# Two-layer hybrid encoder: the attention half of the mixer's output projection is written beside the last steps of the Hyena filters

## The chip, the cores and the metric

The kernel runs on one core of a Trainium2 chip. The metric is device time in microseconds (us), here the median of a few executions. TensorE (PE) multiplies matrices, VectorE (DVE) and ScalarE (ACT) work on elements, GpSimd (POOL) and SyncE (SP) mostly issue DMAs. Each engine works through its own queue in order.

## The reference, cut to what matters

The input is 1024 tokens by 1024 channels, all float32. Layer 0 mixes tokens with two head groups, attention and RWKV-7, whose outputs are concatenated and go through one projection; layer 1 uses a Hyena operator with long filters that depend on weights alone. Each layer ends with a SwiGLU FFN.

```python
def reference(x, c, ...):
    cond = jax.nn.silu(c)
    for layer in range(DEPTH):
        mod = (cond @ ada_w[layer] + ada_b[layer])[:, None, :]
        shift_m, scale_m, gate_m, shift_f, scale_f, gate_f = jnp.split(mod, 6, axis=-1)
        h = rms_norm(x, norm_mix[layer]) * (1.0 + scale_m) + shift_m
        if layer % 2 == 0:
            y = attention_rwkv_mixer(h, ...)   # concat([y_attn, y_rwkv]) @ w_out
        else:
            y = hyena_mixer(h, ...)            # filt = hyena_filters(l, ...) from weights alone
        x = x + gate_m * y
        h = rms_norm(x, norm_ffn[layer]) * (1.0 + scale_f) + shift_f
        x = x + gate_f * swiglu(h, ffn_w1[layer], ffn_w3[layer], ffn_w2[layer])
    return rms_norm(x, final_norm)
```

## The kernel before, in words

**Operands in two parts.** A large product is made of three matmuls with reduced-precision operands (fp32r): each float32 tile is split into a high part (ScalarE copies, L256) and a low part (VectorE subtracts, L257). `mm3` (L296) multiplies high by high, high by low and low by high.

**Pages.** Working memory is cut into pages of 128 partitions by about 1024 columns: float32 pages as a stack from the left, fp32r pages as a stack from the right. `page` takes the page that has been free longest, `free` puts it back. `repage(nf, nr)` changes how many there are of each kind: pages above the new count, which must be free, are given up, and new ones are made in their place. `fence(dt, n)` sorts the free pages into those numbered below n (`pages`) and the others (`beyond`); `zone` says which of the two lists `page` looks at, and in which order. A new page stands where old ones stood, so its first writer waits for the last use of those.

**Order.** The program is written by generators that yield step by step. `weave` takes several with weights and runs always the one whose count of steps over its weight is smallest. The written order is a priority: the scheduler that lays out each engine's queue may put an instruction ahead of others that are written before it, if its data and its page are there first.

**The mixer.** After the input projection `mixer` sets 42 float32 pages and 4 fp32r pages and splits the eight PSUM banks into two groups of four. RWKV's eight units (four head pairs, two directions) pass through three stages, `rwkv_x`, `rwkv_y` and `rwkv_s`, in nine weaves. Beside them runs `other`: attention, in steps of score blocks, and behind it `hy_filters`, which makes the spectra of layer 1's filters in eight quarters (two orders, four column blocks). A quarter loads raw weights (L1788, on POOL), splits them, makes the taps (matmuls L1805, VectorE L1808), multiplies by four DFT matrices that `load_mats` loaded (L1830, VectorE L1750 and L1751), and ends with an eight-point transform (`dft8`, VectorE L1699 and L1700) whose results POOL's queue stores (`hs`, L1777). The transform of a quarter is written beside the taps of the next, and that of the last quarter stands alone at the end. In the last weave (i = 9) only `rwkv_s` of the last unit and `other` (64 steps at most) are left. `rwkv_post` ends it, with L1544 as its last VectorE operation, and spills the RWKV output (`sp_yr`).

**The projection.** Then `build` repages to 13 float32 and 33 fp32r pages, loads x back in eight tiles (`sp_x`), and runs `project`: it loads and splits the four attention outputs (`sp_ya`), and `matvec_add` loads and splits four weights of 512 by 256 (`in_mix_w_out`, L274) and makes eight output tiles of 24 matmuls each. Each tile ends with two gated residual adds (L801). The RWKV half follows in `halves` (`matvec_halves`, L828), woven with the norm ahead of the FFN.

```python
    K.repage(13, 33)
    xT = [K.unspill(d) for d in xd]
    run(project(xT, ys[:4], w[:512], 0))
    xT, steps = K.ffn(xT, halves(xT, ys[4:], w[512:], 0), 0, ada1(), hy_weights(), 20)
```

`project` is also used in `hyena`, where it is woven with the convolutions (`rest`), and there loads and stores each tile of x by itself.

Of the kernel before, what the change touches and what calls it, by code (L numbers as in the profile page):

```python
# [10 lines left out]
F32 = mybir.dt.float32  # L11
# [10 lines left out]
P = 128  # L22
# [41 lines left out]
def run(gen):  # L64
    for _ in gen:
        pass


def some(gen, n):

    for _ in range(n):
        if next(gen, gen) is gen:
            return
        yield


class Kern:
# [77 lines left out]
    def page(self, shape=(P, 1024), dt=F32):  # L155
        t = next(z[dt] for z in self.zone if z[dt]).popleft()
        return reshape(t[:, : int(np.prod(shape[1:]))], shape)

    def free(self, *aps):
        for a in aps:  # L160
            if isinstance(a, (tuple, list)):
                self.free(*a)
            else:
                dt, t, _ = self.page_of[a.tensor.name]
                assert all(t is not q for q in self.pages[dt])
                self.put(t)
# [39 lines left out]
        (eng or self.nc.sync).dma_start(out=d, in_=t)  # L206
        return d

    def unspill(self, d, eng=None):
        t = self.page()  # L210
        (eng or self.nc.sync).dma_start(out=t, in_=d)
        return t

# [566 lines left out]
        at, n = groups[-1]  # L780
        return xT, self.matvec_halves(xT, w2[at * P : (at + n) * P, :], ys, layer, 5, low)

    def matvec_add(self, xT, w, ys, layer, part, g=0, keep=None):

        nc = self.nc
        nk = len(ys)
        load = lambda mp: self.load_w(w[mp] if isinstance(w, dict) else w[:, mp * 256 : mp * 256 + 256], nk, 256)
        nxt = load(0)
        for mp in range(KT // 2):
            wt = nxt  # L790
            if mp + 1 < KT // 2:
                nxt = load(mp + 1)
            for m in (2 * mp, 2 * mp + 1):
                o = (m % 2) * P
                away = xT[m].tensor.name not in self.page_of
                x = self.unspill(xT[m]) if away else xT[m]
                ps = [self.bank(g) for _ in range(2)]
                self.mm3(ps, [(wt[0][:, k, o : o + P], wt[1][:, k, o : o + P]) for k in range(nk)], ys)
                for n in range(2):
                    xs = x[:, HALVES[n]]  # L800
                    nc.vector.scalar_tensor_tensor(out=xs, in0=ps[n], scalar=self.modc(layer, part, m), in1=xs, op0=ALU.mult, op1=ALU.add)  # L801
                self.fbank(ps)
                if keep is not None:
                    keep.append(x)
                elif away:
                    nc.sync.dma_start(out=xT[m], in_=x)
                    self.free(x)
                yield
            self.free(wt)
# [737 lines left out]
        self.free(y)  # L1547
        return d

    def mixer(self, w, h, ada):  # L1550

        self.rwkv_consts()
        self.set_banks(5, 3)

        units = [{"d": d, "hp": hp} for hp in range(4) for d in range(2)]
        self.scanm = self.page((P, PAGE))
        self.nc.sync.dma_start(out=self.scanm, in_=self.ins["k_scanm"])

        def first():

            while (0, "t") not in self.ready:
                yield "wait"
            yield from self.rwkv_x(units[0], 1)

        tiles = self.rwkv_tiles()
        for i, t in zip((13, 15, 17, 19, 20, 21), self.attn_tiles()):
            tiles.insert(i, t)
        out, ys, outr = {}, {}, {}
        att = self.attention(out, 1)

        def begin():

            while (2 not in self.qd) or units[0].get("W") is None or len(units[0]["W"]) < 2:
                yield
            self.zone = (self.beyond, self.pages)
            next(att)
            self.zone = (self.pages,)
            yield
            next(att)
            yield  # L1580

        begun = begin()
        weave((250, self.stream(w, h, tiles, begun)), (60, ada(1)), (30, first()))
        run(begun)
        for a in h:
            self.free(a)
        self.repage(42, 4)
        self.set_banks(4, 4)

        def beside():  # L1590
            f = self.hy_filters(1)
            for n, _ in enumerate(att):
                yield
                if n in (208, 228, 248):
                    next(f)
            yield from f

        other = beside()
        for i in range(1, len(units) + 2):
            if i == len(units):  # L1600
                self.free(self.scanm)
            n = (0, 46, 37, 37, 37, 37, 37, 36, 35, 64)[i]
            gens = [(n, some(other, n))]
            if i > 1:
                gens.append((23 if i <= len(units) else 34, self.rwkv_s(units[i - 2], ys, outr, 0)))
            if i <= len(units):
                gens.append((36, self.rwkv_y(units[i - 1], 0)))
            if i < len(units):
                gens.append((16, self.rwkv_x(units[i], 0)))
            weave(*gens)  # L1610
        for _ in other:
            pass
        self.set_banks(8)
        return [out[i] for i in range(4)] + [outr[i] for i in range(4)]

# [50 lines left out]
            yield  # L1668
        return hid

    def load_mats(self, name):

        out = []
        for i in range(2):
            t = self.page((P, 4, 256))
            self.nc.gpsimd.dma_start(out=t, in_=self.ins["k_" + name][:, 4 * i : 4 * i + 4, :])
            out.append(t)
        return out
# [75 lines left out]
    def hy_filters(self, g):  # L1754

        nc, i = self.nc, self.ins
        hid = yield from self.hy_hidden(g)
        F = self.load_mats("F") + self.load_mats("Fn")
        tneg = self.const("tneg")
        fo = i["hy_f_out"][0]  # L1760
        self.hspec = {}
# [153 lines left out]
    def hyena(self, w, h, tail):  # L1915
# [140 lines left out]
        def rest():  # L2056
            yield from f
            for a in h:
                self.free(a)
            while len(zs) < 4:  # L2060
                yield
            for n, _ in enumerate(tail(zs[:4])):
                yield 1.0 if n == 0 else 5.3

        f = front()
        run(piece(f))
# [28 lines left out]
def build(ctx, tc, ins, out):  # L2095
    K = Kern(ctx, tc, ins)
    spec = [
        ("c", rows(ins["c"])),
        ("ada_b", rows(ins["ada_b"])),
        ("norm_mix", rows(ins["norm_mix"])),  # L2100
        ("norm_ffn", rows(ins["norm_ffn"])),
        ("final_norm", rows(ins["final_norm"])),
    ]
    K.repage(38, 7)
    cols = K.load_cols(spec + K.attn_spec() + K.rwkv_spec() + K.hy_spec())
    next(cols)
    K.ada_init()
    xT = []

    def ada(g):  # L2110
        for m in range(KT):
            xd.append(K.spill(xT[m], f"sp_x0{m}"))
            K.free(xT[m])
            yield
        for part in range(2, 6):
            yield from K.ada_part(0, part, g, 2)

    def ada1():
        for part in range(6):
            yield from K.ada_part(1, part, 0, 2)  # L2120

    def hy_weights():

        w = ins["hy_w_in"][0]
        for j in range(24):
            hw_in[j * P] = K.presplit(w[:, j * P : (j + 1) * P], KT, P, f"hwi{j}")
            yield
        w = ins["hy_w_out"][0]
        for a in range(2):
            for mp in range(4):  # L2130
                hw_out[a][mp] = K.presplit(w[a * 512 : a * 512 + 512, mp * 256 : mp * 256 + 256], 4, 256, f"hwo{a}{mp}")
                yield

    hw_in, hw_out = {}, ({}, {})

    xd = []
    K.load_xT(ins["x"][0], xT)
    K.ada_first()

    def project(xT, ys, w, layer, g=0):  # L2140

        y = [K.split(K.unspill(d)) for d in ys]
        yield
        yield from K.matvec_add(xT, w, y, layer, 2, g)
        K.free(y)

    def halves(xT, ys, w, layer):

        return K.matvec_halves(xT, w, [K.split(K.unspill(d)) for d in ys], layer, 2)

    K.repage(20, 26)
    low = [K.page(dt=F32R) for _ in range(10)]
    h = K.norm_h(xT, 0, 0, [(n, m) for n in range(2) for m in range(KT)], KT - 1)
    K.free(low)
    run(cols)
    w = ins["mix_w_out"][0]
    ys = K.mixer(ins["mix_w_in"][0], h, ada)
    K.repage(13, 33)
    xT = [K.unspill(d) for d in xd]
    run(project(xT, ys[:4], w[:512], 0))  # L2160
    xT, steps = K.ffn(xT, halves(xT, ys[4:], w[512:], 0), 0, ada1(), hy_weights(), 20)

    xd = [K.dram(f"sp_x1{m}") for m in range(KT)]
    h = K.norm_h(xT, 1, 0, steps, 1, xd)
    K.free(xT)
    K.repage(26, 20)
    ys = K.hyena(hw_in, h, lambda y: project(xd, y, hw_out[0], 1))
    K.repage(13, 33)
    xT = [K.unspill(d) for d in xd]
    xT, steps = K.ffn(xT, halves(xT, ys, hw_out[1], 1), 1)  # L2170
    K.final(xT, steps, out)
    K.free(xT)
    K.close()
# [82 lines left out]
```

## Time and profile before

| | us |
|---|---|
| median of 3 runs | 3384.54 (3375.49 to 3385.33) |
| the profiled execution | 3373.19 |
| its span, first to last instruction | 3371.4 |
| mean granted TensorE clock | 0.963 of full speed |

The profile is of one execution. The page gives the busy time of each engine over the whole span. The views used below are windows (busy time of each engine between two times, with the count of instructions, then the granted TensorE clock, the busy share of the DMA engines and the rate), the chain of waits that ended last (start, length, what it was), and the timeline (start, length, engine, line, operation, output and inputs, count; in brackets the idle time of that engine before it, and what ended it).

### The profile page before, as it was taken

What the parts mean: (1) busy time and instruction counts of PE and PEld (TensorE: products, weight loads), DVE (VectorE), ACT (ScalarE), POOL (GpSimd) and SP (SyncE); (2) the same over time, 40 slices, a digit from 0 to 9 for tenths busy, and PEclk for the clock granted to TensorE, in tenths of its full rate; (3) what the DMA queues carried; (4) which work ended last, traced back from release to release, by engine and by line L of the source; (5) the groups of instructions that cost most, each with busy time, mean ns of one, the idle gap of its engine ahead of it and who ended that gap; (6) DMA issues with size and microseconds to landing.
All of it is one profiled execution on the core that took longest, in us unless ns stands there. A gap on an engine that the chain in (4) does not pass through costs nothing.

```text
span 3371.4 us, 51166 instructions
## 1 busy us (share of the span) xinstructions
PE 3158.1 (94%) x20227; PEld 2554.1 (76%) x20227; DVE 2341.6 (69%) x4011; ACT 1229.9 (36%) x2146; POOL 197.0 (6%) x443
## 2 busy tenths in 40 slices
PE   8899989999989979999999999989977899999998
PEld 4687767776668867888887877877765788888886
DVE  5465565666667895887877665699898686667545
ACT  4632355555554432532233333222120443334211
POOL 2000000000001110000001210000000000000000
PEclk9999999989989999999999999999988999999998
DMA  8654542332334253244449983332446322234311
GB/s 273 220 190 139 158 98 70 84 87 64 76 72 111 98 183 137 94 156 137 147 135 308 352 281 125 100 119 90 148 162 218 132 82 75 77 111 138 122 41 51
DMA packets 331377, 460.24 MB, mean 137 GB/s; under 512 B 101816, under 2 KB 233745, under 8 KB 331136
## 3 DMA queue, kind: packets, MB, share of 16 engines
q1 hardware_dynamic: 292576, 322.04, 31.1%
q0 software_dynamic: 38384, 134.86, 11.4%
q8 instruction: 159, 2.61, 0.3%
q14 instruction: 82, 0.67, 0.1%
q10 hardware_dynamic: 176, 0.07, 0.0%
HBM read 312.71 MB, written 141.56 MB: 135 GB/s over the span
## 4 chain that ended last, share of the span: by engine, by line
PE 58%; DVE 8%; DMA 5%; issue 3%; ACT 2%; POOL 0%; DVEq 0%; SPq 0%; ACTq 0%; POOLq 0%
PE bk L296 21%; PE bk L615 8%; PE bk L616 8%; PE bk L614 8%; PE bk L1830 2%; DVE p L1699 2%; PE bk L1849 2%; DMA p<-in_hy_w_in_dram 1%; DVE p L257 1%; DMA p<-in_ffn_w_dram 1%; PE bk L2002 1%; PE bk L1859 1%; PE bk L1805 1%; PE bk L2025 1%; DMA p<-sp_z 1%
## 5 line engine op out<-in xcount | busy, mean ns | idle before, releaser
L296 PE MATMUL bk<-p,p 128*128 128x512 f32 x5136 | 1235.2, 399 | 75.3 <-ACT p L256 35.0
L296 PEld LDWEIGHTS bk<-p,p 128*128 128x128 f32 x5136 | 974.8, 192 | 299.1 <-ACT p L256 39.3
L256 ACT ACTIVATE p<-p 128x512 fp32r<-128x512 f32 (+3 forms) x542 | 402.6, 758 | 945.8 <-PE bk L615 262.4
L257 DVE TENSOR_TENSOR p<-p,p 128x512 fp32r<-128x512 f32 (+3 forms) x542 | 450.9, 847 | 235.0 <-ACT p L256 189.5
L615 PE MATMUL bk<-p,p 128*128 128x512 f32 x1248 | 485.4, 389 | 3.8 <-DVE p L257 3.8
L614 PE MATMUL bk<-p,p 128*128 128x512 f32 x1248 | 485.0, 390 | 0.1
L616 PE MATMUL bk<-p,p 128*128 128x512 f32 x1248 | 483.8, 389 | 0.0
L615 PEld LDWEIGHTS bk<-p,p 128*128 128x128 f32 x1248 | 234.3, 188 | 53.0 <-DVE p L257 4.7
L614 PEld LDWEIGHTS bk<-p,p 128*128 128x128 f32 x1248 | 234.3, 188 | 48.6 <-ACT p L256 0.5
L616 PEld LDWEIGHTS bk<-p,p 128*128 128x128 f32 x1248 | 234.2, 188 | 48.5
L801 DVE SCALAR_TENSOR_TENSOR p<-bk,mod,p 128x512 f32<-128x512 f32 x192 | 134.9, 744 | 95.0 <-PE bk L296 91.7
L443 DVE SCALAR_TENSOR_TENSOR p<-p,cond,p 128x512 f32<-128x512 f32 x140 | 104.6, 749 | 53.6 <-DMA p<-in_ada_w_dram 51.8
L1699 DVE TENSOR_TENSOR p<-p 128x256 f32<-128x256 f32 (+1 forms) x336 | 130.8, 452 | 0.0
L1830 PE MATMUL bk<-p,p 128*128 128x256 f32 x512 | 125.3, 392 | 5.1 <-DVE p L1751 4.0
L944 DVE TENSOR_REDUCE mx<-bk 128x1 f32<-128x512 f32 x128 | 86.2, 684 | 35.5 <-PE bk L941 34.8
L1830 PEld LDWEIGHTS bk<-p,p 128*128 128x128 f32 x512 | 95.1, 194 | 19.6 <-DVE p L1751 5.1
L1056 ACT COPY p<-bk 128x512 f32<-128x512 f32 (+1 forms) x80 | 43.4, 588 | 169.2 <-DVE p L1876 63.9
L1699 DVE TENSOR_TENSOR p<-p,p 128x1024 f32<-128x1024 f32 (+1 forms) x144 | 91.1, 681 | 18.8 <-ACT p L1850 18.8
L964 ACT COPY p<-bk 128x512 f32<-128x512 f32 x128 | 74.2, 587 | 78.4 <-PE bk L963 75.9
L948 ACT ACTIVATE p<-bk,mx 128x512 f32<-128x512 f32 x128 | 86.9, 686 | 42.3 <-DVE mx L945 41.8
L963 PE MATMUL bk<-k_ident,p 128*128 128x128 f32 x512 | 88.3, 300 | 11.8 <-ACT p L964 9.2
L1362 PEld LDWEIGHTS bk<-p,p 64*64 64x64 f32 x2048 | 73.4, 139 | 29.7 <-issue 15.8
(407 smaller groups left out, 4179.9 us busy)
## 6 DMA issues: line engine op xcount, KB each, us to landing
p<-in_ffn_w_dram SPq DMA_DIRECT2D x120, 512.0 KB, 4.8
p<-in_ada_w_dram SPq DMA_DIRECT2D x96, 512.0 KB, 5.0
sp_f<-p POOLq DMA_DIRECT2D x36, 512.0 KB, 5.5
p<-sp_f POOLq DMA_DIRECT2D x36, 512.0 KB, 5.7
hs<-p POOLq DMA_DIRECT2D x32, 512.0 KB, 3.7
p<-hs SPq DMA_DIRECT2D x32, 512.0 KB, 4.4
p<-sp_r SPq DMA_DIRECT2D x24, 512.0 KB, 5.7
p<-sp_x SPq DMA_DIRECT2D x24, 512.0 KB, 3.6
```

Source lines behind the costliest of these rows:

```text
L256: self.nc.scalar.activation(out=hi, in_=src, func=AF.Copy)
L257: self.nc.vector.tensor_tensor(out=lo, in0=src, in1=hi.bitcast(F32), op=ALU.subtract)
L296: nc.tensor.matmul(ps[n], a, b[:, HALVES[n]], start=s, stop=e)
L443: nc.vector.scalar_tensor_tensor(out=acc, in0=wt[:, i], scalar=self.cond[:, k : k + 1], in1=acc, op0=ALU.mult, op1=ALU.add)
L614: nc.tensor.matmul(ps, op[:, 0, k], mh, start=start and k == 0, stop=False)
L615: nc.tensor.matmul(ps, op[:, 0, k], ml, start=False, stop=False)
L616: nc.tensor.matmul(ps, op[:, 1, k], mh, start=False, stop=stop and k == 3)
L801: nc.vector.scalar_tensor_tensor(out=xs, in0=ps[n], scalar=self.modc(layer, part, m), in1=xs, op0=ALU.mult, op1=ALU.add)
L948: nc.scalar.activation(out=pr[:, HALVES[n]], in_=ps[n], func=AF.Exp, scale=0.125, bias=m[:, 2:3], accum_out=st["s", qt // 4][:, qt % 4, e, ...
L963: nc.tensor.transpose(pt[:, j], pr[:, k * P : (k + 1) * P], self.ident)
L1699: tt = lambda o, a, b, op: nc.vector.tensor_tensor(out=o, in0=a, in1=b, op=op)
L1830: nc.tensor.matmul(ps[j][:, ri], F[2 * d + t2 // 4][:, t2 % 4, 128 * ri : 128 * ri + 128], tp[:, j, d], start=d == 0, stop=d == 1)
```

## The change

- `low_page` is new: it takes the free float32 page with the lowest number. `load_mats` takes it for the filters' DFT matrices, and `unspill` for x where the projection asks for it.
- In the last weave (i = 9) `fence(F32, 32)` keeps the pages from 32 up aside; `page` takes them only if there is none below. `other` gets 48 steps in it and no longer 64.
- After that weave `repage(32, 16)` turns the upper pages into twelve more fp32r pages, while the filters are not at their end.
- `build` hands the projection to `mixer` as `tail`. Its first six steps (four splits of attention outputs, two output tiles with the weights that they take) are woven with the rest of `other`, at weights 6 and 16. The rest of it runs after `repage(13, 33)`.
- x is no longer loaded in eight tiles ahead of the projection: `matvec_add` loads each tile at its step, and keeps it (`keep`).
- `project` yields after each split and no longer once after four. In `hyena` the first four steps of it count 0.3 each, where the first step counted 1.0.

```diff
+    def low_page(self, shape=(P, 1024), dt=F32):
+
+        free = self.pages[dt]
+        t = min(free, key=lambda q: self.page_of[q.tensor.name][2])
+        del free[next(i for i, q in enumerate(free) if q is t)]
+        return reshape(t[:, : int(np.prod(shape[1:]))], shape)
...
-    def unspill(self, d, eng=None):
-        t = self.page()
+    def unspill(self, d, eng=None, low=False):
+        t = self.low_page() if low else self.page()
...
-    def matvec_add(self, xT, w, ys, layer, part, g=0, keep=None):
+    def matvec_add(self, xT, w, ys, layer, part, g=0, keep=None, low=False):
...
-                x = self.unspill(xT[m]) if away else xT[m]
+                x = self.unspill(xT[m], low=low) if away else xT[m]
...
-    def mixer(self, w, h, ada):
+    def mixer(self, w, h, ada, tail):
...
-            n = (0, 46, 37, 37, 37, 37, 37, 36, 35, 64)[i]
+            n = (0, 46, 37, 37, 37, 37, 37, 36, 35, 48)[i]
+            if i > len(units):
+
+                self.fence(F32, 32)
+                self.zone = (self.pages, self.beyond)
...
-        for _ in other:
-            pass
+        self.zone = (self.pages,)
+        self.repage(32, 16)
+        last = tail([out[i] for i in range(4)])
+        weave((16, other), (6, some(last, 6)))
         self.set_banks(8)
-        return [out[i] for i in range(4)] + [outr[i] for i in range(4)]
+        return last, [outr[i] for i in range(4)]
...
-    def load_mats(self, name):
+    def load_mats(self, name, low=False):
...
-            t = self.page((P, 4, 256))
+            t = (self.low_page if low else self.page)((P, 4, 256))
...
-        F = self.load_mats("F") + self.load_mats("Fn")
+        F = self.load_mats("F", True) + self.load_mats("Fn", True)
...
             for n, _ in enumerate(tail(zs[:4])):
-                yield 1.0 if n == 0 else 5.3
+                yield 0.3 if n < 4 else 5.3
...
-    def project(xT, ys, w, layer, g=0):
-
-        y = [K.split(K.unspill(d)) for d in ys]
-        yield
-        yield from K.matvec_add(xT, w, y, layer, 2, g)
+    def project(xT, ys, w, layer, g=0, keep=None):
+
+        y = []
+        for d in ys:
+            y.append(K.split(K.unspill(d)))
+            yield
+        yield from K.matvec_add(xT, w, y, layer, 2, g, keep, keep is not None)
         K.free(y)
...
-    ys = K.mixer(ins["mix_w_in"][0], h, ada)
+    xn = []
+    last, ys = K.mixer(ins["mix_w_in"][0], h, ada, lambda y: project(xd, y, w[:512], 0, 0, xn))
     K.repage(13, 33)
-    xT = [K.unspill(d) for d in xd]
-    run(project(xT, ys[:4], w[:512], 0))
-    xT, steps = K.ffn(xT, halves(xT, ys[4:], w[512:], 0), 0, ada1(), hy_weights(), 20)
+    run(last)
+    xT, steps = K.ffn(xn, halves(xn, ys, w[512:], 0), 0, ada1(), hy_weights(), 20)
```

## The prediction

> **What bounds the kernel now.** I read the page first.
>
> ```profile
> PE 3158.1 (94%) x20227; PEld 2554.1 (76%) x20227; DVE 2341.6 (69%) x4011; ACT 1229.9 (36%) x2146; POOL 197.0 (6%) x443
> ```
>
> TensorE is busy for 94% of the span, so 213 us (3371.4 less 3158.1) is all that can be won by filling its gaps, and each gap has to be looked up in its place. The changed place was found in the order of time: the last transform of the filters (L1699, L1700) just before the first matmuls of the projection (L296). I cut that stretch into windows at the starts and ends of a few instructions (PE, PEld, DVE, ACT, POOL busy; granted clock, DMA share, GB/s):
>
> ```profile
> 1228.29:1253.01 24.72, 19.14 (x114) 15.30 (x112) 23.51 (x47) 4.78 (x6) 2.12 (x4) 0.93 0.60 209
> 1253.01:1263.33 10.32, 0.00 (x1) 0.00 (x0) 10.32 (x17) 3.17 (x3) 1.16 (x3) 0.67 0.96 377
> 1263.33:1271.34 8.01, 7.05 (x18) 5.14 (x19) 8.01 (x18) 2.11 (x2) 0.38 (x1) 0.58 0.95 340
> 1271.34:1275.49 4.15, 1.59 (x8) 0.97 (x7) 3.58 (x4) 3.18 (x3) 0.68 (x2) 1.00 1.03 387
> 1275.49:1281.00 5.51, 5.45 (x16) 4.02 (x17) 2.73 (x3) 3.02 (x3) 0.00 (x0) 0.69 0.95 323
> 1281.00:1344.37 63.37, 63.37 (x283) 52.50 (x281) 31.49 (x42) 11.87 (x18) 0.00 (x0) 1.00 0.23 78
> ```
>
> The reader is to see two stages. Up to 1271 VectorE is full (41.84 of 43.05 us) and TensorE idles: 5.58, then 10.32, 0.96 and 2.56 us, 19.4 in all. From 1275.5 on TensorE is full and VectorE half idle. Work of TensorE that can go from the second stage into the first is won, as far as VectorE can feed it. The chain of waits shows the seam:
>
> ```profile
> 1268.82 5.54 DMA p<-sp_ya
> 1274.38 1.06 ACT p L256
> 1275.47 1.24 DVE p L257
> 1276.75 67.62 PE bk L296 x290
> ```
>
> The end goes through the load of the last attention output and its split, then through matmuls alone. The order of time (timeline) says why that load is late:
>
> ```profile
> 1241.83 9.58 SPq L211 DMA_DIRECT2D p<-sp_x  x5
> ...
> 1251.90 1.06 ACT L256 ACTIVATE p<-p 128x1024 fp32r<-128x1024 f32 x1 [12.52 <-DVE p L1544]
> 1252.25 0.54 SPq L211 DMA_DIRECT2D p<-sp_ya  x1
> 1252.98 1.22 DVE L257 TENSOR_TENSOR p<-p,p 128x1024 fp32r<-128x1024 f32 x1 [1.17 <-ACT p L256]
> ...
> 1254.72 0.68 DVE L1751 SCALAR_TENSOR_TENSOR p<-p,bk 128x512 f32<-128x512 f32 x1
> 1255.32 2.35 DVE L1699 TENSOR_TENSOR p<-p,p 128x1024 f32<-128x1024 f32 x2
> ...
> 1258.44 1.06 ACT L256 ACTIVATE p<-p 128x1024 fp32r<-128x1024 f32 x1 [5.49 <-DMA p<-sp_ya]
> 1260.14 1.21 DVE L257 TENSOR_TENSOR p<-p,p 128x1024 fp32r<-128x1024 f32 x1
> ...
> 1263.33 2.07 PE L296 MATMUL bk<-p,p 128*128 128x512 f32 x4 [10.32 <-ACT p L256]
> ...
> 1266.37 6.56 PE L296 MATMUL bk<-p,p 128*128 128x512 f32 x20 [0.96 <-DVE p L257]
> ...
> 1268.71 2.63 DVE L1700 SCALAR_TENSOR_TENSOR p<-p,p 128x256 f32<-128x256 f32 x6
> ```
>
> The queue holds five loads of x ahead of the first attention output, and the first split of the projection waits 12.52 us for L1544, the last operation of the last RWKV head pair: only then is there a page for its operand. One tile of the projection (4 and 20 matmuls, 24 in all) still gets in before the filters end at 1271.3.
>
> That split is written behind the whole filter generator and yet runs before the final transform. So the order on an engine is not the written one: an operation goes in where its data and its page are there, and the written order decides among those that are ready. This carries much of what follows.
>
> **The change, part by part.** *Twelve more operand pages and early operands.* The ten pages from 32 up are no longer taken in the last weave unless the others run out, and are turned into operand pages (16 instead of 4) while filter steps are left. Counting yields in the source, 60 filter steps are left when the last weave begins: 8 of the fourth filter quarter, 4 times 12, and 4 of the last transform. The weave takes 48 of them, so 12 stand beside the projection. At weights 16 and 6 the four splits are written after the 1st, 3rd, 6th and 8th of these, tile 0 with its two weight loads after the 11th, and tile 1 at the end. RWKV's last scan (23 steps at weight 34) ends by the written order after 32 filter steps in place of 43, so its pages, and the page that L1544 releases, come free sooner.
>
> What it takes to start tile 0 is the weight's split and the first attention split; the three others may follow, 1.21 us of VectorE apart, while six matmuls run on each. If they go in as the weight's did before (1252.98, ended 1254.2), the start t0 is 1254.2. If the operations of the last taps and the first transform step go between, it is 1259 (five splits are 6.1 us, L1750 and L1751 1.2). I take 1257, nearer to the trace of before, which let the weight in at 1252.98.
>
> From t0 on the eight tiles can run without a gap: the second weight is split beside tile 0, the third finds pages that the filters' own operands leave, and tile 2 takes the banks of tile 0 again (the projection has RWKV's four, the filters keep theirs). A tile lasts as long as two residual adds are apart:
>
> ```profile
> 1304.74 1.41 DVE L801 SCALAR_TENSOR_TENSOR p<-bk,mod,p 128x512 f32<-128x512 f32 x2 [4.03 <-PE bk L296]
> 1310.18 1.41 DVE L801 SCALAR_TENSOR_TENSOR p<-bk,mod,p 128x512 f32<-128x512 f32 x2 [4.03 <-PE bk L296]
> 1315.17 0.63 ACT L256 ACTIVATE p<-p 128x512 fp32r<-128x512 f32 x1 [21.43 <-PE bk L296]
> ```
>
> That is 5.44 us, 0.227 for a matmul. The 20 matmuls at 1266.37 took 6.56 instead of 4.53, and the 16 from 1275.49 took 5.51 instead of 3.63: the granted clock was 0.58 and 0.69 there, after idle time, and each such start loses about 2 us. Before, the eighth tile ends at about 1315.2 (1275.49 + 7 x 5.44 + 1.9 = 1315.5). After, it ends at t0 + 8 x 5.44 + 2.0 = 1302.5. **Gain: 12.7 us.** With t0 between 1248 and 1268 it is 21.7 to 1.7.
>
> The Trainium skill, "TensorE: Matmul & The Clock Gate", section "Part 1: The HAM clock gate", says that an idle window of some 3.4 us puts the array at half rate and a busy one of that length restores it. The windows agree in kind (0.67 and 0.58 after 10.32 idle us). By its figures a cold start costs an estimated 1.7 us, and the sum would be 12.9, or up to 1.7 more if no window goes idle at all.
>
> *VectorE* pays by being later with the filters: before, five splits of the projection stand ahead of their end; after, six (four outputs, two weights) and the adds of two or three tiles, 1.21 + 3 x 1.41 = 5.4 us more. From 1253 on nothing of TensorE waits for the filters' end but pages for later weights, so I price this at nothing; if that cover fails (tile 4 starts at 1257 + 2 + 21.8 = 1281, four us after the filters' new end), it costs what it is late, up to 5.4.
>
> *Loads of x* go one by one beside their tiles and no longer ahead of the attention outputs. The add needs them, not the matmuls: nothing. If a bank waits for an add that waits for x, up to the 5.54 of the load in the chain.
>
> *Fewer pages in the last weave.* Counted in the source, 18 of 42 pages are free at its start, 13 of them below 32. A shorter round means that a page is asked for sooner after its release. Below: nothing, since VectorE has a backlog; above: the stalls that the rivals price. I take 1.5 us.
>
> *Low pages for the filters' four matrices.* They were loaded and first used at:
>
> ```profile
> 1001.71 0.57 POOL L1676 DMA_DIRECT2D p<-in_k_Fn_dram  x1 [4.08 <-PE bk L1418]
> ...
> 1017.84 0.53 POOL L1676 DMA_DIRECT2D p<-in_k_Fn_dram  x1
> ...
> 1032.25 3.72 PE L1830 MATMUL bk<-p,p 128*128 128x256 f32 x16
> ```
>
> Between the last issue and the first use are 14.4 us, enough for a later page: nothing. If that cover is gone, the nearest price is the load in the chain, 5.54, and the filters' raw weights, queued behind on POOL, come as much later.
>
> *Hyena's projection* yields once for each split (four times 0.3 where one step cost 1.0). Its start, and what VectorE does there:
>
> ```profile
> 2504.02 5.38 PE L296 MATMUL bk<-p,p 128*128 128x512 f32 x12 [4.88 <-ACT p L256]
> ...
> 2518.41 10.70 PE L296 MATMUL bk<-p,p 128*128 128x512 f32 x36 [9.01 <-ACT p L256]
> ```
>
> ```profile
> 2500.00:2510.00 10.00, 5.38 (x12) 3.80 (x12) 8.99 (x11) 3.26 (x4) 0.00 (x0) 0.66 1.08 408
> 2510.00:2520.00 10.00, 1.59 (x4) 1.16 (x4) 9.96 (x14) 1.97 (x2) 0.00 (x0) 0.63 0.85 301
> ```
>
> TensorE waits 13.9 us for the splits, but VectorE works 18.95 of the 20: nothing. The bounds are 13.9 gained and 9.0 (one more such wait) lost.
>
> *Does the gain last?* The next stages are full of matmuls, and where DMA is full, TensorE is still nearly so:
>
> ```profile
> 1500.00:1600.00 100.00, 100.00 (x455) 83.22 (x454) 78.50 (x130) 30.56 (x52) 2.12 (x4) 1.00 0.42 137
> 1800.00:1850.00 50.00, 47.67 (x209) 38.44 (x210) 32.16 (x39) 16.48 (x17) 10.96 (x21) 1.00 1.07 359
> ```
>
> So what is won at 1302 moves all that follows. Sum: 12.7 - 1.5 = 11.2, about **11 us**. The profiled execution took 3373.2 us, 1.8 more than its span, so 3362 would be its like. It lies 11 below the shown median of 3384.5; from that the forecast is **3373.5 us**.
>
> **The rivals.** *Written order holds.* Tile 0's weights are written after the third of the four last transform steps. If VectorE keeps to that, their split is not ahead of L1700 at 1268.7, t0 is 1270, the eighth tile ends at 1315.5, and nothing is won: 3384. Against it stands the split at 1252.98. *Page shortage, slower.* Filter pages go round faster, and POOL issues a quarter's stores and the next quarter's weights in order. The chain has shown such a stop twice:
>
> ```profile
> 1087.18 10.70 issue
> ...
> 1101.77 9.92 issue
> ```
>
> Then VectorE runs dry by up to 10.7 us in a quarter, and since it bounds this stage each counts in full. From two such stops in the five quarters of the last weave on it is slower: 20.6 - 11 = 9.6, 3394. For it: 13 low pages instead of 18. Against: RWKV's pages come back early in this weave, and the reserve of high ones still stands. *Hyena moves.* Its two waits vanish or one is added: gain 25 or 2, 3360 or 3382. *Operands come earlier than I think*: t0 at 1248 or before, since the scan's pages fall free well ahead of L1544; gain 20, 3364.
>
> **How the numbers follow.** Forecast (gain 5 to 17) 0.50, written order 0.16, page shortage 0.11, hyena 0.13, earlier operands 0.10. About 0.3%, 10 us, is what a measurement here can tell from no change (three runs of before lie 9.8 apart). Faster by more: 0.31 of the forecast's half, the early case's 0.10, hyena's better half 0.06, so 0.47. Slower: the shortage with two stops or more, 0.10. Same: 0.43. The range takes the forecast's, the written order's and most of the early case: 3360 to 3387.
>
> **What would show it.** Right: the profile after has the projection's first 128x512 matmuls (L296, one line or several later) before 1260, no idle stretch of 10 us ahead of them, the chain without the load of sp_ya, and eight tiles that end some 12 us sooner against the same filters. x loads follow the attention loads. Wrong: TensorE idle until the last transform is done (written order); VectorE with holes between 1120 and 1250, released by POOL's loads or stores (shortage); a projection that starts early but with gaps between tiles 2 and 5, for weights or banks; or the first stage as forecast and the difference in the hyena stretch.

## The result, and the profile after

| | before | changed |
|---|---|---|
| median of 5 runs, us | 3384.54 (3373.95 to 3385.33) | 3361.86 (3356.45 to 3369.29) |
| ratio to before, 95% interval | | 0.9945 [0.9927, 0.9964] |
| the profiled execution, us | 3373.19 | 3360.89 |
| its span, us | 3371.4 | 3359.1 |

The changed kernel is faster by 0.55%: 18.6 us of 3384.5, with an interval of 12 to 25. The two profiled executions are 12.3 apart. The ratio is not that of the two medians, which lie 22.7 apart. Two later comparisons gave 0.9956 [0.9941, 0.9971] and 0.9953 [0.9934, 0.9971]. One execution of the changed kernel in the last of them took 5248.4 us at a granted clock of 0.587 and counts in no figure here.

The same stretch in windows, cut at the changed kernel's own seams (PE, PEld, DVE, ACT, POOL busy; granted clock, DMA share, GB/s):

```profile
1228.29:1247.70 19.41, 16.76 (x116) 14.38 (x114) 19.41 (x37) 6.78 (x9) 1.06 (x2) 1.00 0.35 124
1247.70:1255.30 7.60, 0.13 (x2) 0.00 (x1) 6.22 (x14) 1.06 (x1) 1.06 (x2) 0.83 0.97 352
1255.30:1268.40 13.10, 13.10 (x51) 10.82 (x51) 7.81 (x9) 3.17 (x4) 0.10 (x1) 0.84 0.67 226
1268.40:1281.00 12.60, 12.60 (x57) 10.46 (x56) 11.72 (x16) 3.93 (x4) 1.06 (x2) 1.00 0.84 283
```

TensorE now idles for 2.65 and 7.47 us, 10.1 where it idled for 19.4, and is full from 1255.3 instead of 1275.5. The chain of waits of the changed kernel (start, length, what) shows which wait took the old one's place:

```profile
1247.85 6.25 DMA p<-in_mix_w_out_dram
1254.19 1.06 ACT p L263
1255.30 3.78 PE bk L303 x8
1259.08 2.01 PE bk L1844 x8
1261.09 5.93 PE bk L303 x26
1267.02 1.73 PE bk L1844 x8
1268.75 64.38 PE bk L303 x284
```

It goes no longer through an attention output but through the projection's first weight. Of the 7.47 us that TensorE idles just before 1255.3, 6.25 are the transfer of that weight, while the DMA engines are busy for 0.97 of the time. In the changed kernel L303 is `mm3`, L263 and L264 the split, L1844 the filters' DFT, L1714 the last lines of the transform, L808 the residual add. In the order of time:

```profile
1219.87 8.14 SPq L218 DMA_DIRECT2D p<-sp_ya  x4
...
1224.26 1.06 ACT L263 ACTIVATE p<-p 128x1024 fp32r<-128x1024 f32 x1 [1.71 <-DMA p<-sp_ya]
...
1234.71 1.21 DVE L264 TENSOR_TENSOR p<-p,p 128x1024 fp32r<-128x1024 f32 x1
...
1245.70 0.86 SPq L218 DMA_DIRECT2D p<-sp_x  x2
...
1247.85 0.39 SPq L281 DMA_DIRECT2D p<-in_mix_w_out_dram  x1
...
1262.31 1.23 DVE L264 TENSOR_TENSOR p<-p,p 128x1024 fp32r<-128x1024 f32 x1 [5.21 <-ACT p L263]
...
1286.51 2.63 DVE L1714 SCALAR_TENSOR_TENSOR p<-p,p 128x256 f32<-128x256 f32 x6
...
1306.28 1.40 DVE L808 SCALAR_TENSOR_TENSOR p<-bk,mod,p 128x512 f32<-128x512 f32 x2
```

The last line is the eighth tile's pair of adds. Before, it was:

```profile
1315.62 1.41 DVE L801 SCALAR_TENSOR_TENSOR p<-bk,mod,p 128x512 f32<-128x512 f32 x2 [4.03 <-PE bk L296]
```

The four attention outputs are loaded from 1219.9 and split by 1235.9, 40 us earlier than the last of them before (1276.7), and well ahead of RWKV's last operation (L1551, at 1249.0). TensorE still has to wait: the weight stands behind two x loads and one load of an RWKV output (`sp_yr`) in SyncE's queue (SPq). The waits of that queue (who waited for whom: total, times, longest; L218 loads x and the mixer's outputs, L281 weights):

```profile
SPq L218 <- PE bk L1844: 16.1, 2, 14.0
SPq L281 <- PE bk L1844: 0.7, 1, 0.7
```

An x load had to wait 14.0 us until the filters' matmuls had read the page that it was to fill, and the weight was queued behind it. But when its turn came, the weight (L281) waited another 0.7 us for the same matmuls, so its own page was no earlier free. The queue alone did not hold it back.

**Where the difference lies.** One stretch can be read in every profile: from the first tap matmul of the filters to the first FFN matmul. Rows by line, before and then changed (first and last start after the three durations in ns):

```profile
L1805 PE MATMUL bk<-p,p x256: 274/282/682, 1025.7 to 1234.2; 128*128 128x256 f32 x128
...
L614 PE MATMUL bk<-p,p x1248: 388/389/501, 1361.0 to 3099.3; 128*128 128x512 f32 x179
```

```profile
L1819 PE MATMUL bk<-p,p x256: 274/282/682, 1026.0 to 1237.6; 128*128 128x256 f32 x128
...
L621 PE MATMUL bk<-p,p x1248: 388/389/501, 1349.8 to 3088.9; 128*128 128x512 f32 x179
```

It takes 335.3 before and 323.8 after: 11.5 of the 12.3 us between the two spans. From the first FFN matmul to the end of the span they take 2010.4 and 2009.3. The first tap falls at a different time in every profile, so times in different runs are best counted from it.

### The profile page after: what moved, and what is told of

The parts are those of the page before. It is cut to its first block, busy times and chain, and to the rows that moved or that the text cites. A ratio compares the mean times of both kernels' runs of the same rounds, so it can differ in the third digit from the quotient of the medians.

```text
span 3359.1 us, 51180 instructions
## 1 busy us (share of the span) xinstructions
PE 3149.6 (94%) x20227; PEld 2547.2 (76%) x20227; DVE 2339.5 (70%) x4011; ACT 1227.9 (37%) x2146; POOL 197.0 (6%) x443
## 4 chain that ended last, share of the span: by engine, by line
PE 57%; DVE 9%; DMA 5%; issue 2%; ACT 2%; POOL 0%; DVEq 0%; ACTq 0%; SPq 0%; POOLq 0%
PE bk L303 21%; PE bk L622 8%; PE bk L621 8%; PE bk L623 8%; DVE p L1713 2%; PE bk L1844 2%; PE bk L1863 2%; DMA p<-in_hy_w_in_dram 1%; DVE p L264 1%; PE bk L2016 1%; DMA p<-in_hy_w_out_dram 1%; DMA p<-in_ffn_w_dram 1%; PE bk L1873 1%; PE bk L2039 1%; PE bk L1819 1%
## 5 line engine op out<-in xcount | busy, mean ns | idle before, releaser
L303 PE MATMUL bk<-p,p 128*128 128x512 f32 x5136 | 1232.9, 399 | 73.0 <-ACT p L263 32.4
L303 PEld LDWEIGHTS bk<-p,p 128*128 128x128 f32 x5136 | 972.8, 191 | 295.2 <-ACT p L263 36.3
L263 ACT ACTIVATE p<-p 128x512 fp32r<-128x512 f32 (+3 forms) x542 | 401.2, 758 | 933.5 <-PE bk L622 248.5
L264 DVE TENSOR_TENSOR p<-p,p 128x512 fp32r<-128x512 f32 (+3 forms) x542 | 451.2, 848 | 255.5 <-ACT p L263 211.7
L808 DVE SCALAR_TENSOR_TENSOR p<-bk,mod,p 128x512 f32<-128x512 f32 x192 | 134.8, 744 | 71.4 <-PE bk L303 68.3
L1844 PE MATMUL bk<-p,p 128*128 128x256 f32 x512 | 122.6, 386 | 4.1 <-DVE p L1822 1.7
L1844 PEld LDWEIGHTS bk<-p,p 128*128 128x128 f32 x512 | 93.7, 190 | 18.6 <-DVE p L1822 2.3
```

Source lines behind the costliest of these rows:

```text
L263: self.nc.scalar.activation(out=hi, in_=src, func=AF.Copy)
L264: self.nc.vector.tensor_tensor(out=lo, in0=src, in1=hi.bitcast(F32), op=ALU.subtract)
L303: nc.tensor.matmul(ps[n], a, b[:, HALVES[n]], start=s, stop=e)
L1844: nc.tensor.matmul(ps[j][:, ri], F[2 * d + t2 // 4][:, t2 % 4, 128 * ri : 128 * ri + 128], tp[:, j, d], start=d == 0, stop=d == 1)
```

## The experiments

All were built from the two kernels and timed beside before on their own chip. "Stretch" is the one just defined.

| run | ratio to before, 95% interval | stretch, us |
|---|---|---|
| before, first and second profile | 1 | 335.3, 336.0 |
| x by tile | 0.9981 [0.9970, 0.9993] | 324.6 |
| x by tile, 48 steps | 1.0004 [0.9991, 1.0018] | 339.6 |
| pages only, 64 steps | 0.9974 [0.9961, 0.9986] | 328.4 |
| pages only (48 steps) | 0.9947 [0.9928, 0.9965] | 325.5 |
| pages only without the fence | 0.9990 [0.9975, 1.0005] | 335.5 |
| changed, first and second profile | 0.9945, 0.9956 | 323.8, 323.6 |
| changed, Hyena as before | 0.9943 [0.9927, 0.9959] | 325.3 |
| changed, first weight ahead | 0.9931 [0.9916, 0.9947] | 314.5 |
| the same, again | 0.9911 [0.9887, 0.9935] | 316.3 |
| changed, two weights ahead | 0.9940 [0.9919, 0.9961] | 320.4 |

**x by tile.** The kernel before, with x loaded tile by tile:

```diff
-    xT = [K.unspill(d) for d in xd]
-    run(project(xT, ys[:4], w[:512], 0))
+    xT = []
+    run(project(xd, ys[:4], w[:512], 0, 0, xT))
```

> The kernel before, with one edit: x is no longer loaded in eight tiles ahead of the projection, each tile is loaded at its step and kept. No page is made earlier, nothing is written beside the filters. Theory (operand pages made early let TensorE start the projection beside the filters): the first projection matmul stays near 1263, the four attention loads come 5 to 10 us sooner, the 2.6 us gap at 1271 to 1275 goes, gain 0 to 4 us. Rival (the order of the x loads alone held the attention outputs back): gain 8 us or more, most of what the change brings.

(`project` hands the last argument on as `keep`.) It is 6.4 us faster (2 to 10), and its stretch is 10.7 shorter. Neither theory hits the timed gain: more than the gap at 1271, less than the whole. By the stretch it brings nearly all that the whole change brings (324.6 against 323.8 and 323.6). Its timeline, with line numbers as in the kernel before:

```profile
1226.81 0.32 SPq L211 DMA_DIRECT2D p<-sp_ya  x1
...
1248.43 0.80 SPq L211 DMA_DIRECT2D p<-sp_ya  x2
...
1259.97 1.06 ACT L256 ACTIVATE p<-p 128x1024 fp32r<-128x1024 f32 x1 [4.99 <-DVE p L1544]
1261.08 11.85 PE L296 MATMUL bk<-p,p 128*128 128x512 f32 x48
```

Counted from the first tap, the first attention load comes 30 us sooner, a split still waits for RWKV's last operation (L1544), and then two tiles run in a row (48 matmuls) before the filters end, though nothing of the projection was written beside the filters.

**Hyena as before.** In the changed kernel, `project` yields once behind its four splits in Hyena, and that step counts 1.0:

```diff
-                yield 0.3 if n < 4 else 5.3
+                yield 1.0 if n == 0 else 5.3
```

> The changed kernel, with Hyena's projection as before: it yields once after its four splits, and that step counts 1.0. Theory: the gain is all in the mixer's end, so this is within 2 us of the changed kernel, 15 to 20 us faster than before by the timed runs and about 12 by the profiles. Rival (part of the gain beyond the forecast 11 us is Hyena's): 5 to 9 us slower than the changed kernel.

No difference: 0.9943 beside the changed kernel's 0.9945. In the profiles, the matmuls of Hyena's transforms (L2025 before, L2039 in the changed kernel), between which its projection runs, take from the first to the last 387.7 us before, 388.2 in the changed kernel and 387.8 here. The gain is not Hyena's.

**Pages only.** The changed kernel, with the filters written to their end first:

```diff
-        self.repage(32, 16)
-        last = tail([out[i] for i in range(4)])
-        weave((16, other), (6, some(last, 6)))
+        for _ in other:
+            pass
+        last = tail([out[i] for i in range(4)])
```

> The changed kernel, but the filters run to their end before the projection begins to be written, and no operand pages are made until then: it keeps the fence at 32, the 48 steps, the low pages and x by tile. Theory: close to the run with x by tile alone, 0 to 4 us faster than before less 1.5 us for the shorter round of pages. Rival (page shortage costs more than the 1.5 us taken): 5 us or more slower than x by tile. Rival (the fence and 48 in place of 64 bring the gain by ending the scan sooner): 8 us or more faster than before.

This was the surprise: 0.9947, all of the gain, with no tile written beside the filters. Its first projection matmul:

```profile
1237.90 1.06 ACT L263 ACTIVATE p<-p 128x1024 fp32r<-128x1024 f32 x1 [2.14 <-DMA p<-sp_ya]
...
1257.79 2.08 PE L303 MATMUL bk<-p,p 128*128 128x512 f32 x4 [9.04 <-ACT p L263]
```

starts 1.4 us later than the changed kernel's, counted from the first tap, and the first split shown waits for its data alone. By the source, the `repage(13, 33)` written behind the filters makes its operand pages over the upper pages too; the fence keeps these free, so they can be written early. Which page each split took is not in the profile.

**The first weight ahead.** In the changed kernel, the first weight is loaded and split before the attention outputs:

```diff
+        first = K.load_w(w[:, :256], len(ys), 256) if keep is not None else None
         for d in ys:
             y.append(K.split(K.unspill(d)))
             yield
-        yield from K.matvec_add(xT, w, y, layer, 2, g, keep, keep is not None)
+        yield from K.matvec_add(xT, w, y, layer, 2, g, keep, keep is not None, first)
```

> The changed kernel, with the projection's first weight loaded and split ahead of the four attention outputs in the written order. In the changed kernel's trace the four splits of attention outputs are done at 1235.9, and the first matmul waits until 1255.3 for the weight, issued at 1247.85 behind two x loads that waited 14 us for a page. Theory: the first matmul comes at 1236 to 1242, the filters' last matmuls are no longer held up behind it, and the kernel is 4 to 8 us faster than the changed one. Rival (VectorE bounds this stage, so an earlier start of TensorE is given back later): within 2 us of the changed kernel.

(`matvec_add` takes `first` in place of its own first load.) The first projection matmul starts at 1235.8, at the early end of what was expected, and TensorE is full where it had idled:

```profile
1228.00:1240.00 12.00, 12.00 (x76) 10.82 (x75) 11.52 (x17) 5.99 (x8) 0.11 (x1) 1.00 0.79 264
1240.00:1250.00 10.00, 10.00 (x71) 8.19 (x70) 10.00 (x22) 4.81 (x7) 0.95 (x2) 1.00 0.64 214
1250.00:1260.00 10.00, 10.00 (x46) 8.44 (x45) 10.00 (x18) 0.08 (x1) 1.03 (x3) 1.00 0.46 159
1260.00:1270.00 10.00, 7.88 (x36) 6.37 (x35) 7.94 (x12) 2.12 (x2) 0.12 (x1) 1.00 1.03 357
```

The stretch is 9.3 shorter than the changed kernel's. It is the fastest kernel here. The edit moves two things at once, the weight's place in the queue and the page that it takes; no run parts them.

**48 steps, and the fence, each alone.** Two runs complete a square with "x by tile" and "pages only". In "x by tile":

```diff
-            n = (0, 46, 37, 37, 37, 37, 37, 36, 35, 64)[i]
+            n = (0, 46, 37, 37, 37, 37, 37, 36, 35, 48)[i]
```

and the same line the other way, in "pages only":

```diff
-            n = (0, 46, 37, 37, 37, 37, 37, 36, 35, 48)[i]
+            n = (0, 46, 37, 37, 37, 37, 37, 36, 35, 64)[i]
```

> The run with x by tile (0.9981 of before), with one more edit: the last weave takes 48 filter steps in place of 64, the rest of them come behind it. With the two runs there are (x by tile; pages only, 0.9947) this and the next make a square of two edits. Theory A (the fence frees pages of high number early, and operands made over them can be written before the filters end): like x by tile, 0.997 to 0.999. Theory B (ending the scan 11 filter steps sooner frees pages and VectorE sooner): 0.994 to 0.996, most of the way to pages only.

> The run with pages only (0.9947 of before), with one edit back: the last weave takes 64 filter steps again. It keeps the fence at 32, the low pages for the filters' matrices, x by tile and Hyena's yields. Theory A (the fence): 0.994 to 0.996, like pages only. Theory B (the scan that ends sooner): 0.997 to 0.999, like x by tile.

The square is not a sum. Without fence, 48 steps cost what x by tile had won (0.9981 to 1.0004); with it they win (0.9974 to 0.9947). With 64 steps the fence, and the low pages that come with it in these runs, are worth nothing over x by tile: the intervals overlap, and the stretch is 3.8 longer (328.4 against 324.6). Theory B falls: without the fence the scan's last matmuls come 195.9 us after the first tap with 64 steps and 193.9 with 48, RWKV's last operation comes 5.0 sooner, and the kernel is slower. Theory A missed both numbers too: the fence matters, but only together with 48 steps.

The run with the fence and 64 steps shows that an early start is not enough:

```profile
1250.37 1.19 PE L303 MATMUL bk<-p,p 128*128 128x512 f32 x4
...
1265.15 7.52 PE L303 MATMUL bk<-p,p 128*128 128x512 f32 x20 [2.92 <-DVE p L264]
...
1292.53 47.78 PE L303 MATMUL bk<-p,p 128*128 128x512 f32 x199 [4.70 <-ACT p L263]
```

Its projection begins 216.6 us after the first tap, 12.7 sooner than in the changed kernel (229.3), but then TensorE stops five times for splits, 12.8 us in all. In the changed kernel it does not stop again up to the FFN.

What goes wrong without the fence, in the run with 48 steps:

```profile
1277.95 1.06 ACT L256 ACTIVATE p<-p 128x1024 fp32r<-128x1024 f32 x1 [3.48 <-DMA hs<-p]
...
1279.06 3.25 PE L296 MATMUL bk<-p,p 128*128 128x512 f32 x7 [13.66 <-ACT p L256]
```

A split waits for a page until a filter result in it is stored, and TensorE, which had begun the projection at 1263.2, stands for 13.66 us.

**Without the fence.** To part the fence from the low pages, "pages only" without it:

```diff
-            if i > len(units):
-                self.fence(F32, 32)
-                self.zone = (self.pages, self.beyond)
```

> The run with pages only (0.9947 of before), with the fence taken out: 48 steps, low pages for the filters' matrices, x by tile and Hyena's yields stay, and page takes any free page in the last weave. It stands to the run with 48 steps (1.0004) as that with the low pages and Hyena's yields added. Theory (the fence keeps the upper pages free, so that operands made over them can be written while the filters run): 0.998 to 1.001, and operand splits that wait for filter results or stores as with 48 steps. Rival (the low pages or Hyena's yields make the difference): 0.994 to 0.996.

0.9990, and the same picture:

```profile
1275.86 1.06 ACT L263 ACTIVATE p<-p 128x1024 fp32r<-128x1024 f32 x1 [3.66 <-DMA hs<-p]
...
1276.97 63.38 PE L303 MATMUL bk<-p,p 128*128 128x512 f32 x272 [10.10 <-ACT p L263]
```

The stretch is 4.1 shorter than with 48 steps alone (335.5 against 339.6); the ratios do not tell the two apart. So with 48 steps the fence is worth 0.43% by the ratios and 10.0 us by the stretch (335.5 to 325.5), and takes this wait away; low pages and Hyena's yields do not replace it. No run has the fence without the low pages.

**The two kernels again.**

> The changed kernel itself, on the same chip as the two runs beside it. Theory (what was forecast: writing two tiles beside the filters is what wins): 4 us or more faster than pages only's 0.9947, so 0.9935 or less. Rival (the order on the engines follows data and pages, so writing the tiles beside the filters adds nothing to early pages): 0.994 to 0.996, the same as pages only within the interval.

> The kernel before, once more with a profile. The profiled execution of before took 3373.2, 7 to 11 us less than the medians of its other executions. If executions differ by a stretch anywhere in the first 1000 us, the last attention scores end later than 999.8 here by as much as the whole is longer; if the stretch that the change touches differs from execution to execution, the time from there to the first FFN matmul is longer than 361.2.

> The changed kernel, third time, beside the two with weights ahead on one chip. All theories: 0.994 to 0.996 of before; from the first tap to the first FFN matmul 323 to 325 us.

0.9956 and 0.9953: the same as pages only within the intervals, and not the 0.9935 or less that the forecast's theory asked for. By the stretch the tiles written beside the filters are worth 1.8 us at most (325.5 to 323.7); the run with Hyena as before has the same tiles and 325.3, so even that is not clear of chance. The second profile of before took 3365.6 with a stretch of 336.0, the second of the changed kernel 3358.8 with 323.6: in these two the stretch repeats within 0.7 us, and what varies lies ahead of it and behind it. The second profile of before was shorter than the first, so it could not show where the longer executions lose their time. The third run of the changed kernel is used for its ratio alone.

**The best version again, and two weights ahead.**

```diff
-        first = K.load_w(w[:, :256], len(ys), 256) if keep is not None else None
+        first = [K.load_w(w[:, 256 * j : 256 * j + 256], len(ys), 256) for j in range(2)] if keep is not None else []
```

> The run with the first weight ahead (0.9931 of before) once more, on the same chip as the changed kernel. Theory: 3 to 8 us faster than the changed kernel beside it, since the stretch from the first filter tap to the FFN took 314.5 there against 323.8. Rival (given back later in the kernel): within 2 us.

> As the run with the first weight ahead, and the second weight too. With the first alone TensorE is full from 1228 to 1260 but for nothing and loses 2.1 us of 1260 to 1270, where splits wait for later weights. Theory: 0 to 3 us faster than with one weight ahead. Rival (the attention outputs come later behind two weights, 1.2 us of VectorE and one load each): 0 to 4 us slower than with one.

On one chip the medians are 3351.88 with one weight ahead, 3359.17 with two and 3364.52 for the changed kernel. One weight ahead beats the changed kernel by more than the 3 to 8 us expected (the intervals just meet). In the two runs with it the stretch is 314.5 and 316.3, so the same kernel can differ by 1.8 here. Two weights are worse: the medians are 7.3 apart, where the rival had 0 to 4, but the intervals overlap; the stretch is 4 to 6 longer. The first projection matmul comes at 1238.8, and a hole opens at the end of the attention half, whose cause the profile does not show ("issue" is time without a releaser):

```profile
1302.60 30.39 PE L303 MATMUL bk<-p,p 128*128 128x512 f32 x120 [4.46 <-issue]
```

## Why the prediction came out right, and which of its steps did not

- **Direction and size.** 11 us were forecast; the stretch gives 11.5 to 12.4, the spans 12.3, the timed ratios 15 to 19, with intervals that begin near 10 and 12. The first timed gain, 18.6, lies above the forecast's own 5 to 17. What the timed runs show beyond the stretch was not found: the profiled execution of before was at the low end of its runs, and all kernels with low pages gain 1 to 11 us more by the timed ratio than by the stretch, 48 steps without them 3 more, while x by tile gains 4 less. So how the whole gain divides among the edits also stays open: by the stretch x by tile brings nearly all of it, by the timed ratios less than half.
- **The sum met the stretch in part by luck.** It was 12.7 at the eighth tile less 1.5 for fewer pages. At that tile 9.3 came in all, and another 1.9 was won between it and the first FFN matmul, for which the sum has no term.
- **t0.** 1257 forecast, 1255.3 measured. But the reason was wrong in its parts: the attention splits were done some 20 us earlier than taken, and the weight, which I took as the early one because it was so before, came last.
- **The eighth tile.** 12.7 us earlier forecast; its adds start at 1306.28 instead of 1315.62, 9.3 earlier. The missing term is on TensorE: 16 DFT matmuls of the filters are queued behind the projection's first ones and take 2.21 and 1.89 us in the timeline, 4.1 together, within tiles 0 and 1. From the measured t0 the sum gives 1300.8, 5.5 too early, so 1.4 us are left without a name.
- **One cold start in place of two** held: 8 matmuls took 3.78 us instead of 1.82, about 2.0 lost, and the clock is 1.00 from 1268.4. The 1.7 estimated from the Trainium skill, "TensorE: Matmul & The Clock Gate", "Part 1: The HAM clock gate", agrees within 0.3. In the kernel before, though, the second cold start followed only 2.56 idle us (the granted clock was 0.50 from 1277 to 1280), less than the 3.4 us that the section names.
- **VectorE's cover** held, by more than I thought: the filters' last operation starts 17.8 us later (1286.5 against 1268.7; 5.4 forecast), and nothing of TensorE waited for it.
- **"Loads of x: nothing"** was the step that failed most. It asked what a late x costs, not what eight early ones had cost the queue. Alone it brings 6.4 us, and 10.7 in the stretch. It is the only edit of the change that was run all by itself.
- **"Two tiles written beside" as the cause** failed too. I had read in the trace of before that an operation goes in where data and page are there, and yet booked the gain on the written order. Pages only shows that it brings 1.8 us by the stretch at most and nothing that the times can tell.
- **The fence at 1.5 us of cost** had the wrong sign: with 48 steps it takes away a wait of 10 to 14 us, with 64 it (with the low pages) wins nothing that can be measured. Why 48 steps lose without it and win with it is shown only as far as the wait for a stored filter result; which page each operand lands on is not in the profiles.
- **The rivals.** Written order did not hold the weight back to the end. Page shortage did not come: from 1120 to 1240 VectorE is busy for 110.5 of 120 us in the changed kernel, 111.2 before, and from 1180 to 1220 it is full. Hyena moved nothing. Operands did come early, as the fourth rival had it, but t0 did not: it waited for the weight. With that weight loaded first t0 came at 1235.8, and the stretch won 20.8 against before, close to that rival's 20. By the forecast's own sum so early a t0 would have won 33.9. That sum lets the tiles run without a gap from t0 on; here the filters' matmuls run between them, and VectorE is full up to 1260.

## What to carry to other kernels

Where a scheduler fills queues by readiness, work comes early when its memory and its data are there, not when it is written early: look at which page the first operation waits for, and who used it last. Loads that are not needed yet, placed ahead of the operands in an in-order queue, cost what the operands wait, also where the loads themselves seem free. The start of a stage is not its length: a projection that began 12.7 us sooner than the changed kernel's ended later, because its splits came too late. After a wait is removed, the next one can be read off the chain at once: here it was the weight, and moving one load won another 7 to 9 us in a stretch in which the whole change had won 11.5.

## What the runs showed that was not expected

A stage of 330 us repeats from execution to execution within 0.2, 0.7 and 1.8 us in the three kernels that were profiled twice, while whole executions of the kernel before lie between 3366.3 and 3389.4 in 25 runs. The first tap falls anywhere from 1018.9 to 1033.8 in the profiles here, and the part from the first FFN matmul on took 2003.8 and 2010.4 in two profiles of the kernel before. A single pair of profiles tells a stage's gain to about 2 us, and the whole's badly.
